# One TensorE burst for each group of S5 operator work inside a feed-forward layer

## The chip, the cores and the metric

The kernel runs on one core of one Trainium2 chip. The core has five engines that run side by side, each with its own queue of instructions: TensorE (PE, matrix products; the loading of its stationary operand is shown as PEld), VectorE (DVE), ScalarE (ACT), GpSimd (POOL) and SyncE (SP). DMA transfers are started by instructions on the queues of SP and POOL. The metric is the device time of one execution in microseconds, as the median of several runs.

## What is computed

The reference is a trunk of four layers over 512 positions of width 1024. Each layer adds a mixer's output to the stream and then a gated feed-forward layer's. Layers 0 and 3 mix with an S5 state space, layer 1 with gated linear attention, layer 2 with differential attention.

```python
for layer in range(DEPTH):
    h = rmsnorm(x, norm_mix[layer])
    mix = s5_mixer(...) | gla_mixer(...) | diff_attn_mixer(...)
    x = x + mix
    h = rmsnorm(x, norm_ffn[layer])
    x = x + swiglu_ffn(h, ffn_w_gate_up[layer], ffn_w_down[layer])
return rmsnorm(x, norm_final)

def swiglu_ffn(h, w_gate_up, w_down):
    g, u = split(h @ w_gate_up, 2)
    return (silu(g) * u) @ w_down
```

The S5 mixer has 64 groups of 16 channels and 64 complex states. Per group it needs an input operator (from B), an output operator (from C), both scaled by powers of the discrete step, and their product, a short map from inputs to outputs:

```python
bu = einsum('bcgh,gph->bcgp', u_c, bb)          # input operator, real and imaginary part
s  = scan of s * a + bu                         # the recurrence
y  = einsum('bcgp,ghp->bcgh', s_re, c_re) - einsum('bcgp,ghp->bcgh', s_im, c_im)
```

These operators depend on weights alone, so those of layer 3 can be made at any time before it.

## The kernel before

**The feed-forward layer.** `ffn` takes the hidden width of 2816 in 11 blocks of 256. The gate and up products of a block are made as seven products of half size (`seven_block`, TensorE at line 575). Blocks come in groups; in layer 0 these are of 3, 3, 3 and 2 blocks. After each group, `gemm_b` multiplies its activations by the matching rows of the down weights, for the left and then the right half of the output. Every product of full precision is a triple of matmuls with 512 columns (`mm3`, lines 432 to 434). The weights arrive by DMA in the tiles `wst` and `slot`, ScalarE rounds them (line 404), VectorE makes the remainder (line 412), and TensorE hands the buffers back by using them.

**The jobs.** In layer 0 the down products carry a second stream of work, `s5_spilled`: a generator that makes the S5 operators of layer 3 in eight passes, each for 4 of 32 pairs of groups (called a group of blocks here, numbered 0 to 7 by `kk`), and writes them to DRAM. `gemm_b` calls `self.job()` after every triple of matmuls; each call runs the generator to its next `yield`. There are 48 calls in the down products of three blocks, and a pass takes 17 calls. The three stretches of down products after blocks 0-2, 3-5 and 6-8 hold all eight passes. A call's instructions are kept behind the last work of the feed-forward layer on TensorE, ScalarE and VectorE; otherwise the build's planner orders what is ready, engine by engine.

One pass consists of these pieces:

- `s5_loads`: four loads on GpSimd's queue (lines 1105 and 1108): B's two parts in `bb`, C's in `craw`, one buffer each.
- `s5_qt`: TensorE turns C into the bank `cps` (line 1141). This is the burst "C".
- `s5_x`: VectorE makes the input operator X (`pre`, `one`, `two`; lines 1095 to 1097).
- `s5_q`: ScalarE copies the turned C into Q (`base`, line 1162), VectorE makes the powers (`one`, `two`; same lines 1095 to 1097).
- `s5_b_pads`: ScalarE copies a part of X into padded rows (line 1185).
- `s5_xt`: TensorE turns one half (real or imaginary) of X into a bank `xps` (line 1249). Two bursts, one for each half; ScalarE copies each out with two instructions (`diag`, line 1311).
- `s5_rows`: TensorE makes the map's rows in a bank `rps` (line 1203). One burst.
- `s5_map`: VectorE and ScalarE move the map's rows out (lines 1213, 1217), GpSimd's queue writes them to DRAM (line 1219) and reads them back in eight pieces (line 1228).
- three stores to DRAM on GpSimd's queue (lines 1350 to 1352).

So TensorE is taken out of its triples four times a pass: C, first half of X, map rows, second half of X. The banks `cps`, `xps` and `rps` all come from one pool of two buffers. The four bursts are plain fp32 matmuls with small tiles (128x64, 64x64, 128x32 of the array), while the triples use the whole array in another number format.

GpSimd's queue also carries loads of the feed-forward layer that add a second weight quarter on the way in (line 611), for the blocks to come.

Of the kernel before, what the change touches and what calls it, by code (L numbers as in the profile page):

```python
# [11 lines left out]
F32 = mybir.dt.float32  # L12
# [9 lines left out]
P = 128  # L22
# [302 lines left out]
class Trunk:  # L325
# [803 lines left out]

        return X, pre, one, two  # L1130

    def s5_qt(self, craw):

        out, n8 = [], craw.shape[2]
        for z in range(2):
            if z * n8 % 4 == 0:
                ps = self.tp("cps")
            at = z * n8 % 4
            for j in range(n8):
                for h in range(2):  # L1140
                    self.nc.tensor.matmul(
                        ps[h * 64 : (h + 1) * 64, at + j], craw[:, z, j], self.ident[:], start=True, stop=True
                    )
            out.append(ps[:, at : at + n8])
        return out

    def s5_q(self, eng, pool, L, b0, nb, bufs=1):


        Q = pool.tile([P, 2, nb, 5, 16], F32, tag="Q", name="Q", bufs=bufs)  # L1150
        f = lambda *r: self.cross(eng, pool, L, b0, nb, *r, "dq")

        def base(ps, vector=None):
            for z in range(2):
                for h in range(2):
                    r = slice(h * 64, (h + 1) * 64)
                    dst = Q[r, z, :, 0].rearrange("p (j b) h -> p j b h", b=4)
                    src = ps[z][r].rearrange("p j (b g h) -> p j b g h", g=2, h=16)[:, :, :, h]
                    if vector:
                        vector.tensor_scalar_mul(dst, src, 1.0 if z == 0 else -1.0)  # L1160
                    else:
                        self.nc.scalar.mul(dst, src, 1.0 if z == 0 else -1.0)

        def one():
            f(1, 4, Q[:, 0, :, 1:5], Q[:, 0, :, 0], Q[:, 1, :, 0], ALU.add)

        def two():
            f(1, 4, Q[:, 1, :, 1:5], Q[:, 1, :, 0], Q[:, 0, :, 0], ALU.subtract)

        return Q, base, one, two  # L1170

# [20 lines left out]
        for _ in range(n):  # L1192
            self.nc.tensor.matmul(ps[:, :P], self.ident[:], self.ident[:], start=True, stop=True)

    def s5_rows(self, nb, bp, Q):

        rp = self.tp("rps")
        rv = rp[:].rearrange("p a b -> p (a b)").rearrange("p (k n) -> p k n", n=64)
        for b in range(nb):
            o = rv[(b % 4) * 32 : (b % 4) * 32 + 32, b // 4]  # L1200
            for z in range(2):
                q = Q[:, z, b, 0:4].rearrange("p j h -> p (j h)")
                self.nc.tensor.matmul(o, bp[:, z, b * 32 : (b + 1) * 32], q, start=z == 0, stop=z == 1)
        return rv
# [89 lines left out]
    def s5_spilled(self, pool, L):  # L1294


        nc = self.nc
        inm = pool.tile([P, 2, 4, 64], F32, name="inmsp")
        mp = pool.tile([P, 4, 64], F32, name="mapsp")
        bp = pool.tile([P, 2, P], F32, name="bpsp")  # L1300
        rs = pool.tile([P, 1, 112], F32, name="rssp")
        self.zero_off(bp, 16)
        nc.gpsimd.memset(rs[:, :, :48], 0.0)
        self.spill = [{} for _ in range(8)]
        self.dq = nc.gpsimd
        raw = self.s5_loads(pool, L, 0, 4)

        def diag(dst, ps):
            for g in range(2):
                r = slice(g * 64, (g + 1) * 64)  # L1310
                nc.scalar.copy(dst[r], ps[r, :, r])

        for kk in range(8):
            bb, craw = raw
            yield
            ps = self.s5_qt(craw)
            X, pre, one, two = self.s5_x(nc.vector, pool, L, 4 * kk, 4, bb)
            pre()
            one()
            yield  # L1320
            yield
            two()
            Q, base, one, two = self.s5_q(nc.vector, pool, L, 4 * kk, 4)
            base(ps)
            yield
            yield
            one()
            self.s5_b_pads(bp, X, True)
            yield
            yield  # L1330
            two()
            if kk < 7:
                raw = self.s5_loads(pool, L, 4 * kk + 4, 4)
            yield
            yield
            x0 = self.s5_xt(X, 0, 0)
            yield
            yield
            diag(inm[:, 0], x0)
            yield  # L1340
            yield
            rv = self.s5_rows(4, bp, Q)
            yield
            x1 = self.s5_xt(X, 1, 0)
            yield
            self.s5_map(L, 4 * kk, 4, rv, rs, mp, True)
            yield
            diag(inm[:, 1], x1)
            d = {w: self.dp.tile([P, n], F32, name=f"{w}{kk}") for w, n in (("in", 512), ("out", 512), ("map", 256))}
            nc.gpsimd.dma_start(d["in"][:], inm.rearrange("p a b c -> p (a b c)"))  # L1350
            nc.gpsimd.dma_start(d["out"][:].rearrange("p (z b n) -> p z b n", z=2, b=4), Q[:, :, :, 1:5].rearrange("p z b j h -> p z b (j h)"))
            nc.gpsimd.dma_start(d["map"][:], mp.rearrange("p b n -> p (b n)"))
            self.spill[kk].update(d)
            yield

    def s5_phases_spilled(self, L):
# [1147 lines left out]
```

## Time and profile before

| what | us |
|---|---|
| median of three runs | 2280.0 |
| the three runs | 2278.26, 2280.0, 2282.13 |
| span of the profiled execution, first to last instruction | 2272.3 |
| busy in it: TensorE | 2198.1 |
| busy: VectorE | 1584.4 |
| busy: ScalarE | 1109.9 |
| busy: GpSimd | 328.0 |

The profile gives the span of its execution and no time beyond it; the median of the timed runs is 7.7 us longer than that span. Rows of groups, waits and stretches name an engine, a line of the kernel, an operation and its tiles (out<-in). "Idle before" is the time that the engine stood still ahead of an instruction, with what ended it. The granted clock is the share of full speed at which TensorE was allowed to run. In the timeline the duration of a matmul includes its run-out, which overlaps the next one; the distance from start to start tells its cost in a stream. An fp32 matmul of the program shows as two records: the C burst is 8 records, a half of X 16, the map rows 16. Tiles of the jobs are shown as `halves`, the memory that they are cut from.

### The profile page before, as it was taken

The numbers are of one execution on the slowest core, as the hardware profiler recorded it, in microseconds if no ns is written. First come the engines' busy times: TensorE is split into PE (matmuls) and PEld (weight loads), VectorE is DVE, ScalarE is ACT, GpSimd is POOL, SyncE is SP. The second block draws the span as 40 slices with busy tenths as digits, with TensorE's granted clock in tenths as the row PEclk, the third lists the DMA queues.
The fourth block names the chain that finished last, engine by engine and source line by source line (L and its number), as shares of the span: only waits on it lengthen the run. The fifth ranks groups of instructions, "written<-read, shape, count | busy, mean of one in ns | idle before, by whom it ended". The sixth has DMA issues, their size and how long they took to land. (4 is left out here: it accounts for less than half of the span.)

```text
span 2272.3 us, 37257 instructions
## 1 busy us (share of the span) xinstructions
PE 2198.1 (97%) x14871; PEld 1955.4 (86%) x14871; DVE 1584.4 (70%) x2413; ACT 1109.9 (49%) x1779; POOL 328.0 (14%) x446
## 2 busy tenths in 40 slices
PE   6999999999999999999999999999999899999998
PEld 5888889889777799998988887999999888989997
DVE  9965878786525488777745676976766965957675
ACT  6634545454443355554435675644534224635343
POOL 6401142421000010100002231110000000101000
PEclk9999999999999999999999999999999999999999
DMA  4356666663322556665247465985641555766622
GB/s 88 64 171 167 166 157 179 163 180 93 114 76 66 153 154 177 181 172 154 94 139 149 98 148 135 230 213 143 170 100 57 141 155 147 194 172 157 168 75 75
DMA packets 294504, 319.92 MB, mean 141 GB/s; under 512 B 70141, under 2 KB 233241, under 8 KB 294202
## 3 DMA queue, kind: packets, MB, share of 16 engines
q1 hardware_dynamic: 231706, 235.79, 34.1%
q0 software_dynamic: 62624, 81.75, 19.4%
q8 instruction: 117, 1.92, 0.3%
q14 instruction: 57, 0.47, 0.1%
HBM read 285.62 MB, written 16.65 MB: 133 GB/s over the span
## 5 line engine op out<-in xcount | busy, mean ns | idle before, releaser
L412 DVE TENSOR_TENSOR whl<-wst,whl 128x1024 fp32r<-128x1024 f32 x272 | 331.9, 1225 | 267.7 <-ACT whl L404 267.0
L404 ACT CAST whl<-wst 128x1024 fp32r<-128x1024 f32 x272 | 284.5, 1051 | 342.5 <-PE acc L434 242.2
L575 PE MATMUL a<-side,whl 128*128 128x256 f32 x3168 | 383.0, 277 | 6.7 <-DVE whl L412 6.0
L575 PEld LDWEIGHTS a<-side,whl 128*128 128x128 f32 x3168 | 370.2, 188 | 8.9 <-DVE whl L412 6.8
L432 PE MATMUL acc<-whl,act 128*128 128x512 f32 x704 | 278.9, 396 | 1.8 <-DVE g L620 1.6
L433 PE MATMUL acc<-whl,act 128*128 128x512 f32 x704 | 275.7, 392 | 0.0
L434 PE MATMUL acc<-whl,act 128*128 128x512 f32 x704 | 275.7, 392 | 0.0
L575 PE MATMUL c<-side,whl 128*128 128x256 f32 x2112 | 254.8, 277 | 3.6 <-DVE whl L412 3.6
L575 PEld LDWEIGHTS c<-side,whl 128*128 128x128 f32 x2112 | 246.6, 188 | 4.5 <-DVE whl L412 4.4
L412 DVE TENSOR_TENSOR whl<-slot,whl 128x1024 fp32r<-128x1024 f32 x105 | 127.9, 1222 | 64.2 <-ACT whl L404 64.1
L432 PEld LDWEIGHTS acc<-whl,act 128*128 128x128 f32 x704 | 132.6, 188 | 31.7 <-DVE g L620 2.0
L434 PEld LDWEIGHTS acc<-whl,act 128*128 128x128 f32 x704 | 132.5, 188 | 27.9
L433 PEld LDWEIGHTS acc<-whl,act 128*128 128x128 f32 x704 | 132.7, 189 | 26.2 <-issue 0.2
L404 ACT CAST whl<-slot 128x1024 fp32r<-128x1024 f32 x105 | 109.9, 1051 | 74.1 <-PE acc L434 28.2
L432 PE MATMUL acc<-whl,hT 128*128 128x512 f32 x352 | 142.1, 404 | 1.5 <-DVE ro L2233 1.5
L434 PE MATMUL acc<-whl,hT 128*128 128x512 f32 x352 | 137.6, 391 | 0.0
L433 PE MATMUL acc<-whl,hT 128*128 128x512 f32 x352 | 137.4, 390 | 0.0
L575 PE MATMUL d<-sides,whl 128*128 128x256 f32 x1056 | 133.6, 283 | 2.6 <-ACT whl L404 2.6
L575 PEld LDWEIGHTS d<-sides,whl 128*128 128x128 f32 x1056 | 128.9, 191 | 3.4 <-ACT whl L404 3.4
L575 PE MATMUL a<-sides,whl 128*128 128x256 f32 x1056 | 128.9, 278 | 1.7 <-DVE whl L412 1.2
L575 PEld LDWEIGHTS a<-sides,whl 128*128 128x128 f32 x1056 | 124.6, 188 | 3.0 <-DVE whl L412 1.4
L611 POOL DMA_DIRECT2D wst<-in_ffn_w_gate_up_dram x44 | 57.1, 1297 | 442.8 <-DMA wst<-in_ffn_w_gate_up_dram 159.6
(458 smaller groups left out, 3930.0 us busy)
## 6 DMA issues: line engine op xcount, KB each, us to landing
wst<-in_ffn_w_gate_up_dram SPq DMA_DIRECT2D x88, 512.0 KB, 4.4
wst<-in_ffn_w_down_dram SPq DMA_DIRECT2D x88, 512.0 KB, 4.4
slot<-in_ffn_w_gate_up_dram SPq DMA_DIRECT2D x69, 512.0 KB, 6.1
wst<-in_ffn_w_gate_up_dram POOLq DMA_DIRECT2D x44, 512.0 KB, 6.0
halves<-in_ffn_w_gate_up_dram SPq DMA_DIRECT2D x42, 512.0 KB, 5.6
wst<-in_s_w_glu_dram SPq DMA_DIRECT2D x32, 512.0 KB, 4.9
wst<-in_gla_w_in_dram SPq DMA_DIRECT2D x24, 512.0 KB, 3.6
wst<-in_diff_w_qkv_dram SPq DMA_DIRECT2D x24, 512.0 KB, 3.7
```

Source lines behind the costliest of these rows:

```text
L404: self.last["high"] = self.nc.scalar.copy(hl[:, 0], w[:])
L412: self.last["low"] = self.nc.vector.tensor_tensor(hl[:, 1], w[:], hl[:, 0].bitcast(F32), op=ALU.subtract)
L432: mm(out, lh, rh, start=first, stop=False)
L433: mm(out, lh, rl, start=False, stop=False)
L434: self.last["mm"] = mm(out, ll, rh, start=False, stop=last)
L575: mm(o, hl[:, x, k, c], side[:, y, k], start=first and not (j or k or n), stop=k == 3 and n == 2, skip_group_check=True,)
L611: nc.gpsimd.dma_start(w[:], left.quarter(*plus, b), accum_op=ALU.add)
```

## The change

Each pass's four bursts become one, and C is turned one pass ahead:

- Ahead of the loop, group 0's C is turned by itself and Q's base copied (`operators(0, ...)`).
- In pass `kk`, X and Q are both made first. Then one step takes a bank `both` from the pool, turns the *next* group's C into it (`s5_qt(raw[1], both)`), turns both halves of X (`s5_xts`, a helper that existed), and makes the map's rows in the third quarter of the same bank (`s5_rows(..., both[:, 2:3])`).
- One ScalarE instruction copies both halves of X out, instead of four.
- After the map's step, Q's base for the next group is copied from the bank (`operators(kk + 1, ps)`). For that Q has two buffers, by the tags `Q0` and `Q1`.
- The loads of the next group are issued after X's second part rather than after Q's.

A pass still takes 17 calls; one call is added ahead of the first. The last pass has no next C. In the order that the build gives, the merged bursts stand 12, 29 and 46 triples into the first stretch, 15 and 32 into the second, 1, 18 and 35 into the third; the first half of X stood at 10, 27, 44, at 13, 30, 47 and at 16, 33.

```diff
-    def s5_qt(self, craw):
+    def s5_qt(self, craw, bank=None):
...
-                ps = self.tp("cps")
+                ps = self.tp("cps") if bank is None else bank
...
-        Q = pool.tile([P, 2, nb, 5, 16], F32, tag="Q", name="Q", bufs=bufs)
+        Q = pool.tile([P, 2, nb, 5, 16], F32, tag=tag, name="Q", bufs=bufs)
...
-        rp = self.tp("rps")
-        rv = rp[:].rearrange("p a b -> p (a b)").rearrange("p (k n) -> p k n", n=64)
+        rp = self.tp("rps")[:] if room is None else room
+        rv = rp.rearrange("p a b -> p (a b)").rearrange("p (k n) -> p k n", n=64)
...
+        def operators(kk, ps):
+            made = self.s5_q(nc.vector, pool, L, 4 * kk, 4, tag=f"Q{kk % 2}")
+            made[1](ps)
+            return made
+
+        yield
+        nxt = operators(0, self.s5_qt(raw[1]))
         for kk in range(8):
-            bb, craw = raw
-            yield
-            ps = self.s5_qt(craw)
+            bb = raw[0]
+            Q, _, q_one, q_two = nxt
+            yield
             X, pre, one, two = self.s5_x(nc.vector, pool, L, 4 * kk, 4, bb)
             pre()
             one()
             yield
             yield
             two()
-            Q, base, one, two = self.s5_q(nc.vector, pool, L, 4 * kk, 4)
-            base(ps)
-            yield
-            yield
-            one()
-            self.s5_b_pads(bp, X, True)
-            yield
-            yield
-            two()
             if kk < 7:
                 raw = self.s5_loads(pool, L, 4 * kk + 4, 4)
             yield
             yield
-            x0 = self.s5_xt(X, 0, 0)
-            yield
-            yield
-            diag(inm[:, 0], x0)
-            yield
-            yield
-            rv = self.s5_rows(4, bp, Q)
-            yield
-            x1 = self.s5_xt(X, 1, 0)
+            q_one()
+            self.s5_b_pads(bp, X, True)
+            yield
+            yield
+            q_two()
+            yield
+            yield
+            yield
+            both = self.tp("cps")
+            if kk < 7:
+                ps = self.s5_qt(raw[1], both)
+            xs = self.s5_xts(X, 0)
+            rv = self.s5_rows(4, bp, Q, both[:, 2:3])
+            yield
+            yield
+            nc.scalar.copy(inm, xs)
+            yield
             yield
             self.s5_map(L, 4 * kk, 4, rv, rs, mp, True)
             yield
-            diag(inm[:, 1], x1)
+            if kk < 7:
+                nxt = operators(kk + 1, ps)
...
+            yield
             yield
```

The helper that it calls, unchanged:

```python
def s5_xts(self, X, b0):
    ps = self.tp("xps")[:].rearrange("p a b -> p (a b)").rearrange("p (z b n) -> p z b n", z=2, b=4)
    for z in range(2):
        for b in range(4):
            for g in range(2):
                r = slice(g * 64, (g + 1) * 64)
                self.nc.tensor.matmul(
                    ps[r, z, b], X[r, z, b0 + b].rearrange("p s c -> p (s c)"), self.ident[r, r],
                    start=True, stop=True,
                )
    return ps
```

More of the change, by code (lines that the diff above doesn't have):

```diff
@@ L1145, in s5_qt, with s5_q @@
         return out
-    def s5_q(self, eng, pool, L, b0, nb, bufs=1):
-        Q = pool.tile([P, 2, nb, 5, 16], F32, tag="Q", name="Q", bufs=bufs)
+    def s5_q(self, eng, pool, L, b0, nb, bufs=1, tag="Q"):
+        Q = pool.tile([P, 2, nb, 5, 16], F32, tag=tag, name="Q", bufs=bufs)
         f = lambda *r: self.cross(eng, pool, L, b0, nb, *r, "dq")
@@ L1193, in warmed, with s5_rows @@
             self.nc.tensor.matmul(ps[:, :P], self.ident[:], self.ident[:], start=True, stop=True)
-    def s5_rows(self, nb, bp, Q):
-        rp = self.tp("rps")
-        rv = rp[:].rearrange("p a b -> p (a b)").rearrange("p (k n) -> p k n", n=64)
+    def s5_rows(self, nb, bp, Q, room=None):
+        rp = self.tp("rps")[:] if room is None else room
+        rv = rp.rearrange("p a b -> p (a b)").rearrange("p (k n) -> p k n", n=64)
         for b in range(nb):
@@ L1306, in s5_spilled @@
         raw = self.s5_loads(pool, L, 0, 4)
[L1308 to L1311, printed above, removed]
+        def operators(kk, ps):
[4 more added lines that the diff above has]
+        nxt = operators(0, self.s5_qt(raw[1]))
         for kk in range(8):
-            bb, craw = raw
+            bb = raw[0]
+            Q, _, q_one, q_two = nxt
             yield
-            ps = self.s5_qt(craw)
             X, pre, one, two = self.s5_x(nc.vector, pool, L, 4 * kk, 4, bb)
```

## The prediction

> **What bounds the kernel now.** I read the page's busy shares, then the waits of TensorE around the first feed-forward layer, then the table of stretches, then the timeline. The page:
>
> ```profile
> PE 2198.1 (97%) x14871; PEld 1955.4 (86%) x14871; DVE 1584.4 (70%) x2413; ACT 1109.9 (49%) x1779; POOL 328.0 (14%) x446
> ```
>
> TensorE is the bound over the whole span. The waits of TensorE from 262 to 575 us:
>
> ```profile
> PE acc L432 <- DVE g L620: 1.6, 1, 1.6
> PE xps L1249 <- ACT halves L1311: 0.5, 1, 0.5
> PE xps L1249 <- DVE halves L1097: 0.3, 1, 0.3
> ```
>
> Two waits there, 0.5 and 0.3 us, belong to the jobs; all other TensorE time of the down products is spent issuing. So what a burst adds to TensorE's queue is added to the kernel's end. The stretches in which the jobs run (the down products of blocks 0-2, 3-5 and 6-8), then two windows of 3.41 us:
>
> ```profile
> 279.98:325.58 45.60, 43.53 (x299) 32.33 (x297) 33.90 (x79) 18.60 (x47) 24.15 (x38) 0.96 0.63 160
> 383.31:424.79 41.48, 41.48 (x298) 31.29 (x297) 32.41 (x77) 17.17 (x45) 28.27 (x48) 1.00 0.52 138
> 482.41:523.39 40.98, 40.43 (x291) 30.69 (x289) 28.17 (x59) 16.30 (x40) 23.69 (x40) 1.00 0.56 135
> 281.68:285.09 3.41, 1.82 (x13) 1.11 (x10) 2.37 (x3) 1.94 (x3) 1.14 (x2) 1.00 0.97 282
> 285.09:288.50 3.41, 3.41 (x10) 2.66 (x9) 2.11 (x4) 1.78 (x3) 0.00 (x0) 0.50 0.58 181
> ```
>
> Columns: window, length, busy time of PE, PEld, DVE, ACT, POOL, granted clock, DMA share, GB/s. TensorE fills the second stretch wholly; VectorE has 9 us free there, GpSimd 13. Each stretch holds 48 job steps of three matmuls.
>
> **What a burst costs.** Four pieces of TensorE's timeline (start, duration, operation):
>
> ```profile
> 296.16 0.40 PE L434 MATMUL acc<-whl,act 128*128 128x512 f32 x1
> 296.49 0.56 PE L1249 MATMUL xps<-ident,halves 64*64 64x64 f32 x10
> 296.98 0.44 PE L1203 MATMUL rps<-halves 128*32 128x64 f32 x14
> 297.35 0.44 PE L1249 MATMUL xps<-ident,halves 64*64 64x64 f32 x6
> 297.73 0.50 PE L432 MATMUL acc<-whl,act 128*128 128x512 f32 x1
> 298.06 0.40 PE L433 MATMUL acc<-whl,act 128*128 128x512 f32 x1
> 298.30 0.39 PE L434 MATMUL acc<-whl,act 128*128 128x512 f32 x1
> ...
> 300.35 0.39 PE L434 MATMUL acc<-whl,act 128*128 128x512 f32 x1
> 300.67 0.66 PE L1141 MATMUL cps<-ident,halves 128*64 128x128 f32 x8
> 301.25 0.51 PE L432 MATMUL acc<-whl,act 128*128 128x512 f32 x1
> 301.60 0.40 PE L433 MATMUL acc<-whl,act 128*128 128x512 f32 x1
> 301.84 0.40 PE L434 MATMUL acc<-whl,act 128*128 128x512 f32 x1
> ...
> 306.64 0.39 PE L434 MATMUL acc<-whl,act 128*128 128x512 f32 x1
> 306.96 0.68 PE L1249 MATMUL xps<-ident,halves 64*64 64x64 f32 x16
> 307.57 0.50 PE L432 MATMUL acc<-whl,act 128*128 128x512 f32 x1
> 307.91 0.39 PE L433 MATMUL acc<-whl,act 128*128 128x512 f32 x1
> 308.14 0.40 PE L434 MATMUL acc<-whl,act 128*128 128x512 f32 x1
> ...
> 310.20 0.39 PE L434 MATMUL acc<-whl,act 128*128 128x512 f32 x1
> 310.52 0.45 PE L1203 MATMUL rps<-halves 128*32 128x64 f32 x16
> 310.90 0.50 PE L432 MATMUL acc<-whl,act 128*128 128x512 f32 x1
> 311.24 0.39 PE L433 MATMUL acc<-whl,act 128*128 128x512 f32 x1
> 311.46 0.39 PE L434 MATMUL acc<-whl,act 128*128 128x512 f32 x1
> ```
>
> Without a burst a triple of matmuls takes (300.35 - 298.30)/3 = 0.683 us, 0.228 a matmul. A burst costs the time from the L434 ahead of it to the next L434, less 0.683: C 0.81, one half of X 0.82, map rows 0.58. Each splits into a body (burst start to the next L432: 0.58, 0.61, 0.38) and an edge (entry 0.32 instead of 0.23, and slow matmuls behind): 0.20 to 0.23, take 0.21. A group of blocks before: 0.81 + 2 x 0.82 + 0.58 = 3.03 us.
>
> The first piece shows what merging does: three runs of two shapes in one burst have bodies 0.49 + 0.37 + 0.38 = 1.24 and one edge; with the same subtraction it costs 1.46. So a merged burst pays its edge once, and each change of shape inside still pays its body's run-out.
>
> **The change, part by part.**
>
> (1) *Four bursts into one*, the same 40 matmul records. Inside are C (0.58), both halves of X in one run, and the map rows (0.38). The X run of 32 has no row. Two bodies in full would be 1.22; the first piece breaks 16 into 10 + 6 at 0.49 + 0.38 against 0.61 unbroken, so joining saves at most 0.26: 0.96. I take the middle, 1.09. Merged: 0.21 + 0.58 + 1.09 + 0.38 = 2.26, saving 0.77 a group. Seven groups have it all: 5.4. Group 0's C stays a burst of its own ahead of everything, and the last group's burst has no C: 2 x 0.82 + 0.58 - (0.21 + 1.09 + 0.38) = 0.54. Together 5.9. Lower end: if only the two X halves gain from joining (at the 0.21 edge alone), 8 x 0.21 = 1.7; upper end: three edges and the 0.26 join in each group, 8 x 0.89 = 7.1. I take 5.9, since the first piece pays for exactly one edge.
>
> The Trainium skill (TensorEngine Tiling, Key Properties) says that changing the tiling mode, not just the tile, drains TensorE. By it alone a group's eight mode changes become four, so half the fixed cost goes. The trace agrees that the inner changes are not free (10 + 6 cost more than 16); taking the whole fixed cost of three bursts as saved would be too much.
>
> (2) *Two waits go* with the separate X bursts: 0.5 + 0.3 = 0.8 us. The first map-row burst is in two pieces before and after (the build order puts a few matmuls between, as the next Q half is late), which cancels.
>
> (3) *One new wait, in group 0.* All of X and half of Q must be made before one point, 12 triples into the stretch, where the first X half was turned after 10. TensorE's tenth triple, and VectorE:
>
> ```profile
> 290.91 0.39 PE L434 MATMUL acc<-whl,act 128*128 128x512 f32 x1
> 291.89 1.22 DVE L412 TENSOR_TENSOR whl<-wst,whl 128x1024 fp32r<-128x1024 f32 x1
> 293.02 0.35 DVE L1097 TENSOR_TENSOR halves<-halves 128x192 f32<-128x192 f32 x1
> 293.90 0.42 DVE L1095 TENSOR_TENSOR halves<-halves,pw 128x256 f32<-128x256 f32 x1
> ```
>
> Group 0 starts late on VectorE, behind the feed-forward work and the weight split of 1.22. X's last piece ended at 293.02 + 0.35 = 293.4; the built order puts two Q products of 0.42 ahead of it: 294.2. TensorE finishes triple 12 at 290.91 + 0.23 + 2 x 0.683 = 292.5, and its C part (0.09 entry, 0.58 body) at 293.2. Wait: 1.0 us, with signalling 1.1. Behind the waiting matmul stands every down product, in order. The first group of the second stretch has its burst at triple 15; there Q's end and the map rows come out about level, and I charge 0.2. Bounds of this part: 0 and 2.5 (X and all of Q, six products of 0.42, before the burst moves).
>
> (4) *C a group ahead, Q in two buffers.* Same loads, same products. Q no longer waits for the store of the last Q; that was hidden before. C's loads move to an earlier point of GpSimd's queue relative to their use. Prices:
>
> ```profile
> 388.66 0.58 POOL L1219 DMA_DIRECT2D rd<-halves  x1
> 391.26 0.56 POOL L1108 DMA_DIRECT2D halves<-in_s_c_im_dram  x1
> 391.80 4.07 POOL L1228 DMA_DIRECT2D halves<-rd  x8
> rd<-halves POOLq DMA_DIRECT2D x8, 56.0 KB, 2.6
> halves<-in_s_c_re_dram POOLq DMA_DIRECT2D x8, 32.0 KB, 2.8
> ```
>
> In the built order most C loads are issued right behind the burst that frees their buffer, a group (17 x 0.683 + 2.26 = 13.9 us) ahead of use. The tightest is C for group 5: it stands behind the map write of group 3, stores and B loads. GpSimd spends 28.27 us of the second stretch on some three groups, 9.4 each; less the eight map reads of 4.07, 5.3 lie between. Burst 3 ends at 383.31 + 15 x 0.683 + 2.26 = 395.8, its map write goes some 3.5 triples later, 398.2; C is issued by 403.5 and landed by 406.3. Burst 4 begins at 383.31 + 32 x 0.683 + 2.26 = 407.4: 1.1 us to spare. Charged 0; bounds 0 and, if the queue runs as late as one set of map reads, 4.
>
> (5) *ScalarE* copies both X halves in one instruction instead of four: it is at 17 of 41 us in the second stretch, so nothing. The weight loads on the sync queue keep their order, and the weight buffers are handed back by TensorE's matmuls, so the next blocks start earlier with it: no other cover to lose.
>
> Sum: -5.9 - 0.8 + 1.1 + 0.2 = -5.4 us. The profiled execution has a span of 2272.3; the median of the three runs, 2280.0, is 7.7 above, which I keep around it: 2266.9 + 7.7 = 2274.6. The runs themselves lie 3.9 apart, so 0.2% (4.6 us) is about what a measurement of this kernel can tell from no change.
>
> **Rivals.**
>
> *A halved clock behind the new wait.* The two windows above show it: 1.82 us of matmul in 3.41, behind a wait of 1.6, and then a window at clock 0.50, which costs half of 3.41, 1.7 us. If the new 1.1 us wait falls in a window with other gaps, the time is 2276.3. Against: 1.1 of 3.41 leaves two thirds busy, and the window that tripped was barely half busy. The Trainium skill (TensorE: Matmul & The Clock Gate, HAM oscillation) warns of idle gaps longer than about 3.4 us; by it a 1.1 us wait never costs clock. This trace disagrees with so wide a gap, its 1.6 us wait being enough.
>
> *Merging saves little.* Only the halves of X gain: 1.7 of part (1) instead of 5.9, so -1.7 - 0.8 + 1.3 = -1.2, 2278.8. For it: the first piece costs 1.46 where separate bursts of its work would cost 0.82 + 0.58 x 14/16 = 1.33. Against: that piece breaks X in two, which the new order doesn't.
>
> *Slower: the burst waits for the last of its inputs.* One mechanism: C comes first in the burst, TensorE takes its queue in order, and C's load is late on GpSimd's queue. For it: 9.4 us of issuing and a 2.6 us landing of the map write before the reads make 12.0 of a 13.9 us group, and only 1.1 us are to spare for group 5. It decides from 10 us in all, say the two C loads that stand behind other work (groups 3 and 5) each 5 us late: -5.4 + 10, 2284.6. Against: in the built order the other five stand first behind a burst, or have a stretch of feed-forward blocks to land in.
>
> *The change not doing what it says*: the built order shows C, X and map rows adjacent on TensorE in every group but for the break in group 0, so I give that none of its own.
>
> **How the numbers follow.** Forecast -5.4, own range 2272 to 2278: 0.66, three quarters of it under 2275.4 (faster by over 0.2%). A larger gain, all edges and no new wait, 7.1 + 0.8 = 7.9 or 2272.1 and less: 0.02. Halved clock 0.07 and little saved 0.08, both within 0.2%. Late C 0.17, slower. Faster 0.50 + 0.02 = 0.52; same 0.16 + 0.07 + 0.08 = 0.31; slower 0.17. The range from 2271 to 2282 takes in the upper bound of (1), the forecast, both middle cases and a C late in two groups, and leaves out most of the late case.
>
> **What would show it.** Seven bursts of about 40 records at a cost near 2.26 each and one of 32 to 33 near 1.68; the second stretch, which trades eleven bursts for two, shorter by about 4 us, the third by 2, the first about level, since it takes over work of the second. TensorE waiting about 1 us for VectorE's X in the first group, and no wait for ScalarE's X copy in the third stretch. It is wrong if a C load releases TensorE, if the merged burst costs over 2.6, if a window after the first burst shows clock 0.50, or if the blocks behind a stretch begin with a wait for a weight split and give the gain back.

## The result and the profile after

The changed kernel takes 2273.04 us (median of five runs, 2270.68 to 2276.05); the kernel before took 2280.47 beside it (five runs, 2278.26 to 2282.93). The ratio is 0.9976, with a 95% interval of 0.9965 to 0.9986. That is 0.24% faster by the medians, over the 0.2% that was forecast, with an interval from 0.14 to 0.35%; the forecast of 2274.6 is 1.6 us above the median. One later run of the changed kernel took 2746.93 us at a granted clock of 0.752, far from all others, and is left out of the medians below. The sum came out; three of its smaller terms, wholly or in part, and the way it was tied to the median did not.

The profiled execution of the changed kernel took 2276.05 us with a span of 2274.3. The busy shares on its page have hardly moved:

```profile
PE 2196.8 (97%) x14871; PEld 1960.0 (86%) x14871; DVE 1582.4 (70%) x2413; ACT 1102.2 (48%) x1755; POOL 327.9 (14%) x446
```

TensorE remains the bound. The table of stretches of the changed kernel: the three stretches of down products, then two windows of 3.41 us (window, length, busy time of PE, PEld, DVE, ACT and POOL, granted clock, DMA share, GB/s):

```profile
282.78:329.94 47.16, 44.30 (x322) 34.33 (x321) 33.09 (x78) 16.09 (x39) 25.16 (x40) 0.93 0.61 155
387.87:425.30 37.43, 37.43 (x259) 30.14 (x257) 32.17 (x77) 14.46 (x37) 26.01 (x45) 1.00 0.54 142
483.23:522.12 38.89, 38.89 (x307) 31.55 (x305) 27.97 (x59) 13.48 (x31) 23.67 (x40) 1.00 0.56 140
293.43:296.84 3.41, 1.73 (x40) 1.24 (x36) 3.34 (x10) 0.82 (x4) 2.92 (x4) 1.00 0.21 32
296.84:300.26 3.42, 3.21 (x21) 2.06 (x22) 1.79 (x10) 0.61 (x2) 1.44 (x2) 0.50 0.96 204
```

Against before the second stretch is 4.05 us shorter (41.48 to 37.43), the third 2.09 (40.98 to 38.89), and the first 1.56 longer (45.60 to 47.16). The last two rows say why the first is longer: a window that was half filled with matmuls, then a window at clock 0.50 (and a second one behind it, to 303.67).

TensorE's timeline of the changed kernel, the second merged burst with the down products around it, then the one of group 0:

```profile
312.26 0.39 PE L434 MATMUL acc<-whl,act 128*128 128x512 f32 x1
312.58 0.66 PE L1141 MATMUL cps<-ident,halves 128*64 128x128 f32 x8
313.17 1.15 PE L1237 MATMUL xps<-ident,halves 64*64 64x64 f32 x32
314.24 0.45 PE L1203 MATMUL cps<-halves 128*32 128x64 f32 x16
314.62 0.50 PE L432 MATMUL acc<-whl,act 128*128 128x512 f32 x1
...
315.19 0.40 PE L434 MATMUL acc<-whl,act 128*128 128x512 f32 x1
```

```profile
293.14 0.66 PE L1141 MATMUL cps<-ident,halves 128*64 128x128 f32 x8
294.32 0.68 PE L1237 MATMUL xps<-ident,halves 64*64 64x64 f32 x16 [0.53 <-ACT halves L1185]
296.02 0.68 PE L1237 MATMUL xps<-ident,halves 64*64 64x64 f32 x16 [1.02 <-DVE halves L1097]
297.05 0.39 PE L1203 MATMUL cps<-halves 128*32 128x64 f32 x2 [0.34 <-DVE halves L1095]
299.37 0.67 PE L1203 MATMUL cps<-halves 128*32 128x64 f32 x14
```

With the prediction's subtraction the first costs 315.19 - 312.26 - 0.68 = 2.25 us. The other merged bursts cost 2.24 to 2.28, the last one, without C, 1.67. In group 0 the burst waits three times, 0.53 + 1.02 + 0.34 = 1.9 us. VectorE at that time:

```profile
293.82 0.35 DVE L1097 TENSOR_TENSOR halves<-halves 128x192 f32<-128x192 f32 x1
294.09 1.22 DVE L412 TENSOR_TENSOR whl<-wst,whl 128x1024 fp32r<-128x1024 f32 x1
...
295.61 0.36 DVE L1097 TENSOR_TENSOR halves<-halves 128x192 f32<-128x192 f32 x1
```

The second wait, 1.02, is for the second half of X: a weight split of 1.22 us stood between the two halves. The third is for Q. The first wait, 0.53, the profile puts down to ScalarE's copy into the padded rows, which ended at 294.18; VectorE's first half of X ended at 294.17, so the profile does not tell the two apart.

### The profile page after: what moved, and what is told of

It is laid out like the page before. It is cut to its first block, busy times and chain, and to the rows that moved or that the text cites. A ratio compares the mean times of both kernels' runs of the same rounds, so it can differ in the third digit from the quotient of the medians.

```text
span 2274.3 us, 37218 instructions
## 1 busy us (share of the span) xinstructions
PE 2196.8 (97%) x14871; PEld 1960.0 (86%) x14871; DVE 1582.4 (70%) x2413; ACT 1102.2 (48%) x1755; POOL 327.9 (14%) x446
```

## The experiments

The theory after the result: the gain is the smaller number of bursts, at a fixed price for leaving and entering the down products; the wait in group 0 takes some of it. Rivals: the gain comes from turning C a group ahead; the price goes with the amount of work and not with the number of bursts; a change of shape inside a burst costs as much as an interruption. Runs said to be of one execution have no spread of their own; what their bursts cost is read from the timeline, where they repeat from group to group. The first four runs tell where the gain sits, the next four what a burst pays for, the last two what the profile of before had hidden.

**Group 0's burst later.** Five more steps ahead of group 0's burst, so that X and Q are made when TensorE comes to it. All later bursts move with it.

```diff
             yield
+            if kk == 0:
+                for _ in range(5):
+                    yield
             both = self.tp("cps")
```

> The changed kernel, with the burst of group 0 alone five triples later (17 into the first stretch instead of 12), the groups behind it five later too. Theory (the merged burst of group 0 waits for VectorE's X, 0.5 and 1.0 us in the changed kernel's profile, with Q's 0.3 behind it, and the two windows at half clock that follow cost another 3.4): none of these waits, no half clock behind the first burst, every merged burst at 2.25, first stretch about 4 us shorter than the changed kernel's 47.2 for the same number of bursts; against the kernel before -9 us, 2271 us, some 2 to 3 us under the changed kernel's median of 2273.0. Rival (the half clock comes from the gaps of the bursts themselves or by chance): half clock in the first stretch again, no time gained.

Measured: 2271.94 us (2269.02 to 2273.17, six runs), ratio to before 0.9965 (0.9953 to 0.9978). TensorE's wait for the jobs in its profile, and the stretches:

```profile
PE cps L1203 <- DVE halves L1095: 0.5, 1, 0.5
```

```profile
279.64:319.00 39.36, 38.39 (x267) 30.51 (x265) 32.70 (x78) 15.74 (x38) 21.88 (x35) 1.00 0.69 176
376.93:416.40 39.47, 39.47 (x314) 31.94 (x313) 30.09 (x71) 13.99 (x34) 28.05 (x47) 1.00 0.63 156
474.34:515.08 40.74, 39.64 (x307) 31.50 (x305) 29.91 (x65) 14.85 (x36) 21.20 (x35) 1.00 0.57 140
```

The wait for X and the window at half clock are gone; a new wait of 0.5 for Q stands in the third stretch, where group 5's burst now comes early. The stretches take 119.57 us together against 123.48. So in the profiles the wait in group 0 and the half clock behind it had their price. In the times little of it is left: by the medians this kernel is 0.3 us below the changed one run beside it, where 2 to 3 were expected. It is faster than before, and it is not shown to be faster than the changed kernel. What takes the gain back behind the stretches was not followed up.

**The changed kernel again**, unedited, for a second profile and a comparison on the same chip.

> The changed kernel as it is, beside the first of these on the same chip. Theory: 2273 us, -7 us against the kernel before, with the wait of about 1 us for X in the first stretch in its profile again; half clock behind it in some executions only.

Measured: 2272.24 us (median of five runs, 2270.38 to 2274.14), ratio 0.9968 (0.9956 to 0.9981). Group 0's burst waits 0.5 + 1.0 + 0.3 again, this time with no window at half clock behind it. Something else shows instead, in the second stretch. GpSimd's timeline of this run, then TensorE's:

```profile
400.03 0.52 POOL L1228 DMA_DIRECT2D halves<-rd  x1 [4.06 <-DMA halves<-rd]
...
404.44 0.56 POOL L1354 DMA_DIRECT2D map<-halves  x1 [1.87 <-DMA halves<-rd]
...
406.78 0.55 POOL L1108 DMA_DIRECT2D halves<-in_s_c_re_dram  x1
407.32 0.55 POOL L1108 DMA_DIRECT2D halves<-in_s_c_im_dram  x1
```

```profile
408.92 0.86 PE L1141 MATMUL cps<-ident,halves 128*64 128x128 f32 x8 [1.76 <-DMA halves<-in_s_c_re_dram]
```

GpSimd stood 4.06 us ahead of the last read of the map and 1.87 ahead of a store, by the profile until earlier map reads had landed; C for group 5 was issued late, and TensorE waited 1.76 us for it with all down products behind. This is the slower rival, in one group. The same two places on GpSimd's queue in the first profile of the changed kernel:

```profile
402.69 0.52 POOL L1228 DMA_DIRECT2D halves<-rd  x1 [2.13 <-DMA wst<-in_ffn_w_gate_up_dram]
...
409.02 0.55 POOL L1108 DMA_DIRECT2D halves<-in_s_c_im_dram  x1
```

There GpSimd lost 2.13 us ahead of the last map read, both C loads were issued by 409.57 (409.02 + 0.55), and the burst at 412.24 did not wait. So the slack of this load is real and small, and sometimes it is used up: of the eight profiles here with C a group ahead, this is the one that shows the wait.

**Four bursts again, C still a group ahead.** The merged burst is cut in four, a triple between each two; the order of the preparation and Q's two buffers stay. For this and two later runs `s5_xts` was given two more arguments, the bank and the part of X to turn.

```diff
             q_two()
             yield
-            yield
-            yield
             both = self.tp("cps")
             if kk < 7:
                 ps = self.s5_qt(raw[1], both)
-            xs = self.s5_xts(X, 0)
+            yield
+            xs = self.s5_xts(X, 0, None, range(4))
+            yield
+            self.s5_xts(X, 0, xs, range(4, 8))
+            yield
             rv = self.s5_rows(4, bp, Q, both[:, 2:3])
-            yield
```

> The changed kernel with C a group ahead, Q in two buffers and one copy of X, but the burst cut into four again: C, each half of X, map rows, one triple of matmuls between. Theory (the gain lies in the number of bursts): C 0.80, X halves 0.82, map rows 0.58, so 3.02 a group as before the change, second stretch back near 41 us, total within noise of the kernel before. Rival (the gain comes from turning C a group ahead and the slack it leaves): second stretch stays at 37.4, about -6 us.

Measured: 2278.77 us (one execution). C costs 0.80, the halves of X 0.82 each, the map rows 0.60: 3.04 a group, as before the change, and the second stretch is back at 40.74 us. C a group ahead saves nothing in a burst; the gain is in the number of bursts.

**Only the halves of X joined**, in the kernel before:

```diff
-            x0 = self.s5_xt(X, 0, 0)
+            xs = self.s5_xts(X, 0)
             yield
             yield
-            diag(inm[:, 0], x0)
+            nc.scalar.copy(inm, xs)
...
-            x1 = self.s5_xt(X, 1, 0)
...
-            diag(inm[:, 1], x1)
```

> The kernel before, with only the two halves of X in one burst and copied out by one instruction: three bursts a group. Theory: the joined X burst costs 0.21 + 1.08 = 1.29 instead of 1.63, 0.34 a group, 2.7 us in all; C and map rows unchanged at 0.80 and 0.58. Rival (the whole gain is in joining X, different shapes gain nothing from standing side by side): 0.77 a group.

Measured: 2277.21 us (one execution). TensorE's timeline, a joined burst and its neighbours:

```profile
309.51 0.39 PE L434 MATMUL acc<-whl,act 128*128 128x512 f32 x1
309.83 1.15 PE L1237 MATMUL xps<-ident,halves 64*64 64x64 f32 x32
...
311.48 0.40 PE L434 MATMUL acc<-whl,act 128*128 128x512 f32 x1
```

It costs 311.48 - 309.51 - 0.68 = 1.29, where two halves cost 1.64. Joining equal shapes gives 0.35 of the 0.79 a group (3.04 less 2.25) that the merging gives; the rest comes from putting different shapes side by side.

**C's burst one triple apart** from the rest:

```diff
             q_two()
             yield
             yield
-            yield
             both = self.tp("cps")
             if kk < 7:
                 ps = self.s5_qt(raw[1], both)
+            yield
             xs = self.s5_xts(X, 0)
```

> The changed kernel with C's burst taken out of the merged burst and put one triple of down products ahead of it; the same 40 records a group. Theory (each burst pays one edge of about 0.21 us on entering and leaving the down products, and a change of shape inside a burst pays only a run-out): C 0.80 and the rest 1.67, together 2.47 a group where the merged burst measured 2.25; seven groups cost 1.5 us more. Rival (a change of shape inside a burst costs as much as an interruption of the down products): nothing is added, 2.25 a group.

Measured: 2275.11 us (one execution). TensorE's timeline:

```profile
306.29 0.39 PE L434 MATMUL acc<-whl,act 128*128 128x512 f32 x1
306.61 0.66 PE L1141 MATMUL cps<-ident,halves 128*64 128x128 f32 x8
...
307.78 0.40 PE L434 MATMUL acc<-whl,act 128*128 128x512 f32 x1
308.11 1.15 PE L1237 MATMUL xps<-ident,halves 64*64 64x64 f32 x32
309.18 0.45 PE L1203 MATMUL cps<-halves 128*32 128x64 f32 x16
...
310.13 0.40 PE L434 MATMUL acc<-whl,act 128*128 128x512 f32 x1
```

0.81 and 1.67, together 2.48 against 2.25: one more burst costs 0.23, where the theory had 0.22.

**Six bursts**: C, X in four runs of 8 records, the map rows, a triple between each two.

```diff
-            yield
-            yield
...
             if kk < 7:
                 ps = self.s5_qt(raw[1], both)
-            xs = self.s5_xts(X, 0)
+            yield
+            xs = self.s5_xts(X, 0, None, range(2))
+            for n in (2, 4, 6):
+                yield
+                self.s5_xts(X, 0, xs, range(n, n + 2))
+            yield
             rv = self.s5_rows(4, bp, Q, both[:, 2:3])
-            yield
-            yield
             nc.scalar.copy(inm, xs)
-            yield
             yield
```

> The changed kernel with the merged burst cut into six: C, four runs of 8 records of X, and the map rows, a triple of down products between each two. Theory (one edge of 0.21 for each burst, and a body): 6 x 0.21 for the edges, 0.58 for C, 4 x 0.38 for X (a run of 16 had a body of 0.61, one of 10 0.49 and of 6 0.37, so about 0.43 for 8 with a run-out, and 0.38 as the low estimate), 0.38 for the map rows: 3.7 to 3.9 a group, 10 to 12 us more than the changed kernel over the eight groups. Rival (the price goes with the records and hardly with the number of bursts): near 3.0, as the four bursts.

Measured: 2285.21 us (one execution), above every run of the kernel before (2275.63 to 2283.12). A group costs 0.80 + 4 x 0.59 + 0.60 = 3.76, within the 3.7 to 3.9 expected. The same 40 records in one, four and six bursts cost 2.25, 3.04 and 3.76: the price goes with the number of bursts.

**One burst, shapes mixed.** The burst stays whole, but X comes in four runs, with a quarter of the map rows behind each.

```diff
-            xs = self.s5_xts(X, 0)
-            rv = self.s5_rows(4, bp, Q, both[:, 2:3])
+            xs = None
+            for n in range(4):
+                if n == 0:
+                    xs = self.s5_xts(X, 0, None, range(2))
+                else:
+                    self.s5_xts(X, 0, xs, range(2 * n, 2 * n + 2))
+                rv = self.s5_rows(4, bp, Q, both[:, 2:3], (n,))
```

> The changed kernel with its one burst kept whole, but X in four runs of 8 records with 4 records of map rows behind each, so that the shape changes eight times inside the burst instead of twice. Rule that a change of shape drains the array: each run has a body of its own, 0.58 for C, 4 x 0.38 for X, 4 x 0.2 for the rows, body 2.9, cost 3.1 a group, 0.85 over the merged burst's 2.25. Rival (changes inside a burst are free, only leaving and entering the down products costs): 2.25, as the merged burst.

Measured: 2285.04 us (one execution), as slow as six bursts. TensorE's timeline:

```profile
309.35 0.39 PE L434 MATMUL acc<-whl,act 128*128 128x512 f32 x1
309.66 0.66 PE L1141 MATMUL cps<-ident,halves 128*64 128x128 f32 x8
310.25 0.45 PE L1238 MATMUL xps<-ident,halves 64*64 64x64 f32 x8
310.63 0.41 PE L1203 MATMUL cps<-halves 128*32 128x64 f32 x4
310.97 0.45 PE L1238 MATMUL xps<-ident,halves 64*64 64x64 f32 x8
...
313.70 0.39 PE L434 MATMUL acc<-whl,act 128*128 128x512 f32 x1
```

It costs 313.70 - 309.35 - 0.68 = 3.67, with no down product inside, against 2.25 for the sorted burst and 3.1 expected. So a burst pays for changes of the array's shape inside it, and not only for interrupting the down products.

Of the 1.42 more, a part is no change of shape. The four records of map rows that stand together here all use one tile of the array: they last 0.41, which is 0.19 from the first start to the last with 0.22 for the last one itself. The 16 together go round four tiles and last 0.45, 0.23 from first to last. Four times 0.19 is 0.53 more than 0.23. The other 0.89, over six more changes, is 0.15 a change; the X runs alone say the same (four bodies of 0.38 against one of 1.07, 0.45 for three more changes). At a burst's ends a change costs a little more: joining the halves of X takes away two ends and saves 0.35, 0.18 each. Counted in changes of shape (each burst has one going in and one coming out):

| kernel | bursts a group | changes of shape a group | cost a group, us |
|---|---|---|---|
| changed | 1 | 4 | 2.25 |
| C apart | 2 | 5 | 2.48 |
| X joined | 3 | 6 | 2.68 |
| four bursts (before, and four again) | 4 | 8 | 3.04 |
| one burst, mixed | 1 | 10 | 3.67 |
| six bursts | 6 | 12 | 3.76 |

From 4 to 12 changes the slope is 1.51 / 8 = 0.19 us a change, and all kernels but the mixed one lie within 0.05 of that line. The mixed burst lies 0.3 above it, since the rows' 0.53 outweigh its cheaper inner changes; the 3.1 expected had taken 0.2 for the body of four map-row records, which measured 0.34.

**A burst of full tiles.** In each group one more burst, of four fp32 matmuls that use the whole array; their result is read by nobody.

```diff
             nc.scalar.copy(inm, xs)
             yield
+            for _ in range(4):
+                nc.tensor.matmul(both[:, 3], self.ident[:], self.ident[:], start=True, stop=True)
             yield
```

> The changed kernel with one more burst in each group, of 4 fp32 matmuls (8 records) that use the whole 128 x 128 array, as the down products do; their result is read by nobody. Theory (the edge of 0.21 comes from a change of the array's shape): no edge, cost about 0.5 (8 records of 128 columns at the C burst's body less its run-out), entry at the stream's 0.23. Rival (the edge comes from the other number format, or from any interruption): 0.80 as C alone, entry 0.32. The eight extra bursts add 4 to 6.4 us.

Measured: 2277.2 us (one execution). TensorE's timeline:

```profile
312.59 0.40 PE L434 MATMUL acc<-whl,act 128*128 128x512 f32 x1
312.82 1.05 PE L1347 MATMUL cps<-ident 128*128 128x128 f32 x8
313.63 0.47 PE L432 MATMUL acc<-whl,act 128*128 128x512 f32 x1
...
314.17 0.40 PE L434 MATMUL acc<-whl,act 128*128 128x512 f32 x1
```

The entry is 312.82 - 312.59 = 0.23, the stream's own spacing, not 0.32. The down product behind starts 0.03 after the burst's last record, where behind the small tiles it starts 0.15 after. The whole costs 0.90, which is nearly eight records at the 0.11 between their starts (0.89). So a burst in the other number format, but of the same shape, pays next to nothing beyond its records for being one: the shape is what costs. The amount expected, 0.5, was wrong, and by the amount alone the rival's 0.80 is nearer; the entry and the spacing decide against it. The 0.5 took the records at C's pace: C's start in pairs 0.007 apart, on two halves of the array, and full tiles one behind the other.

**The kernel before, profiled twice more**, unedited.

> The kernel before, unchanged, profiled a second time. The prediction put 7.7 us around the profiled span, as a constant, while the span of the changed kernel stood only 1.75 us under its own time. Theory: the time around a span is always 1.7 to 1.8 us, and the first profiled execution of the kernel before was itself a fast one, about 2274; another one near the median of 2280 has a span near 2278.5, with the difference in places: waits in the stretches that the first did not have, or more windows at half clock (1.7 us each). Rival: the time around the span is 7 us for this kernel, and the span is again near 2272.

> The kernel before, unchanged, profiled a third time. Same theories as for the second: by the first, span and time are 1.7 to 1.8 us apart and the three stretches together are longer than the 128.06 us of the first profile wherever the time is over 2276; by the rival the span stays near 2272.

Measured: 2280.74 us with a span of 2279.0, and 2280.99 with 2279.3: 1.7 us around the span, as in every other run here. The wait of the jobs in the first of the two, with its first stretch and two windows:

```profile
PE xps L1249 <- DVE halves L1097: 2.5, 1, 2.5
```

```profile
279.76:327.10 47.34, 43.47 (x298) 32.32 (x296) 33.89 (x79) 18.61 (x47) 24.15 (x38) 0.96 0.62 155
...
289.58:292.99 3.41, 1.26 (x19) 1.10 (x20) 3.31 (x12) 2.44 (x7) 2.64 (x3) 1.00 0.25 66
292.99:296.41 3.42, 3.42 (x10) 2.68 (x9) 3.32 (x13) 1.09 (x5) 0.59 (x2) 0.50 0.80 112
```

The kernel before waits 2.5 us for VectorE's X in group 0 (3.0 in the other profile), and the clock halves behind it. The profile that the prediction read showed 0.3 there. In that execution the clock had halved at 285.1 already and TensorE went at half speed for 3.4 us, so it came later to the burst: VectorE's X was turned from 291.63 there and from 291.73 here. The stretches take 130.02 and 129.67 us in these two, 128.06 in the one read. That is 1.6 to 2.0 of the 6.7 to 7.0 us between the spans; most of the rest lies behind the third stretch, in later layers, and was not followed up.

## Why the prediction was right, and where it was not

1. *Four bursts into one, 5.9.* Right in size: 2.25 a group against 2.26 predicted, 1.67 for the last against 1.68. The X run of 32, for which no row existed, has a body of 314.24 - 313.17 = 1.07; the middle that was taken was 1.09. The mechanism was right too. "A merged burst pays its edge once, and each change of shape inside still pays its body's run-out": an inner change cost 0.15 in the mixed burst and a burst's two ends 0.35, which is a run-out and an edge of 0.20. Merging saves three edges and the run-out between the halves of X, 3 x 0.21 + 0.15 = 0.78, and 0.79 was measured. What the prediction did not say is what the edge is paid for: for the change of shape and not for the interruption, since full tiles pay none. The Trainium skill (TensorEngine Tiling (Array Packing), Key Properties) says that a change of the tiling mode drains TensorE. The mixed burst and the full tiles agree; the price beside it is measured here.
2. *Two waits go, 0.8.* Half right. ScalarE's X copy is waited for no longer. VectorE's X still is, so the 0.3 did not go. And the list held a third wait of the down products, 1.6 us for VectorE (line 620), so that not all their other time was issuing; it is there after the change as well (1.0 us).
3. *One new wait in group 0, 1.1 + 0.2.* Wrong in kind. It came, as 0.53 + 1.02 for X and 0.34 more for Q, 1.9 in all, within the bounds of 0 and 2.5. The order on VectorE was the one foretold, a weight split and two Q products ahead of X's last piece. But it was no new one: two of three profiles of the kernel before wait 2.5 and 3.0 us at the same place, and so does that kernel with X joined, 2.6. The point moved two triples later, which gives VectorE more time, and in the profiles the wait is shorter. The term's sign against those two is a gain of 0.6 to 1.1 (2.5 to 3.0 less 1.9). The failing step was to take one profiled execution's 0.3 as the kernel's.
4. *C a group ahead, 0 with bounds 0 and 4.* Right in the first profile; 1.76 us in the second. The load for group 5 was named, and its slack put at 1.1; in the first profile both loads had been issued 2.7 us before the burst, in the second the last of them left 0.8 us after the burst was due (406.78 + 0.32 = 407.10, and 407.32 + 0.55 = 407.87). What ate the slack was GpSimd's waiting behind map reads, 4.06 and 1.87 us. The estimate for group 5 counted issuing and C's own landing, and no such wait.
5. *ScalarE's copies, 0.* Nothing in the profiles speaks against it.

*The sum and the median.* "7.7 above, which I keep around it" failed: 1.7 us lie around a span in every run that has both, so the execution that was profiled, whose own time is not on record, must have taken some 2274 us, 6 less than the median. The forecast survived, since a difference was added to a median. In the stretches the two profiles of the changed kernel stand at 123.48 and 123.40 and the three of before at 128.06, 129.67 and 130.02: 123.44 on average against a median of 129.67, -6.2 us, beside -5.4 predicted and -7.4 by the medians of the times. An estimate from the measured terms: -5.9, -0.5 for ScalarE's copy, -0.6 to -1.1 for VectorE's X and 0.9 for a late C in one profile of two come to -6.1 to -6.6 (half clock in the first stretch, one window a profile on average before and after, cancels). So the size of the forecast rests on the first term, which was right; that the rest came out small is in part luck, as the third term had the wrong sign and the fourth was put at nothing.

*The stretches.* Second 4.05 shorter (about 4 foretold), third 2.09 (2 foretold), first 1.56 longer where it should have been level. In the second profile of the changed kernel the first takes 44.36, and in the two later profiles of the kernel before 47.34 and 47.41, so with its half clock the first profile is level with these two, and the second, without one, 3 us shorter.

*The rival of the halved clock* had 0.07, and its mechanism appeared in the first profile of the changed kernel: two windows at 0.50, 6.8 us, so about 3.4 lost. It did not decide, because the kernel before pays it too in the same stretch, one window in each of its three profiles. The argument against it ("1.1 of 3.41 leaves two thirds busy") was wrong here: several waits fell into one window, and 1.73 of 3.41 us were left. In the second profile the same waits fell into two windows, and the clock stayed. *Merging saves little* is refuted by the 2.25. *The late C* is there in one of two profiles, at a fifth of the 10 us from which it would have decided.

## What to carry to other kernels

Count the changes of tile shape on TensorE, not the bursts: here each cost about 0.15 us in the middle of a burst and 0.18 at its ends, so sort small work by shape and let runs of one shape stand together. Before a wait is booked as new or as gone, look at a second profile of the unchanged kernel: one execution can hide it behind a window at half clock. The gain on the full engine arrived whole here, but turning C earlier spent the slack of a load on another queue, which varies from execution to execution.

## What the runs showed of the hardware

A TensorE clock window did not need to be idle to be followed by half clock. Cut into the 3.41 us windows in which the clock changes, the windows of the first stretch that held 1.26 (before, second profile), 1.35 (X joined), 1.57 (six bursts), 1.73 (changed), 1.82 (before, first profile) and 2.04 us (mixed) of matmul were all followed by one at 0.50; windows with 1.93 (full tiles) and 2.06 (C apart, full tiles) were not. So waits of 0.5 and 1.0 us that share a window were enough, while in the second profile of the changed kernel, where they lie in two windows with 2.58 and 2.38 us of matmul, they were not. The Trainium skill (TensorE: Matmul & The Clock Gate, HAM oscillation) gives idle gaps over about 3.4 us as the case to avoid; these runs disagree, with no single wait above 3.0 us.

But the profile's busy time gives no bound. Two pairs of windows of the changed kernel, away from the jobs, in the columns of the table of stretches:

```profile
252.47:255.88 3.41, 1.68 (x15) 1.48 (x14) 3.36 (x4) 1.85 (x3) 0.00 (x0) 1.00 1.03 317
255.88:259.29 3.41, 3.41 (x31) 3.41 (x32) 3.41 (x5) 1.73 (x2) 1.32 (x1) 1.00 0.58 193
648.42:651.83 3.41, 3.41 (x26) 3.19 (x27) 1.10 (x1) 0.20 (x1) 0.00 (x0) 1.00 0.29 71
651.83:655.24 3.41, 3.41 (x10) 2.63 (x9) 0.00 (x0) 0.00 (x0) 0.00 (x0) 0.50 0.21 82
```

A window with 1.68 us of matmul kept the full clock behind it, and a window that the profile shows as full was followed by half clock. In the full one, 2.2 us belong to matmuls of two columns each (line 1966), which the profile shows as busy throughout. What the clock goes by is not shown here.

The other surprise is that fp32 matmuls among the down products paid no edge for their format: the full-tile burst entered at 0.23 us, the spacing of the stream itself.
